# gMLP of one decoder layer: four value tiles and four u tiles computed as two Strassen units, and the value norm applied in the copy of the turned values

## The chip, the cores and the metric

The kernel runs on one core of one Trainium2 chip. A run's time is the device time of one execution in microseconds (us). The kernel before took 1926.22 us, the median of three runs (1925.88 to 1927.91). Its profile shows one execution of 1926.16 us, whose recorded span is 1924.4 us; the other 1.76 us lie around the span.

Five engines work side by side, each with its own list of instructions in a fixed order: TensorE (PE, with its weight loads PEld), VectorE (DVE), ScalarE (ACT), GpSimd (POOL) and SyncE (SP), which issues the DMAs. An instruction starts when the engine is free and the semaphores that it waits for have come.

## What is computed

Two layers over 544 tokens (512 of a prompt, 32 of eight samples) with a model width of 1024. The change lies in the token mixer of layer 0, a chunked gMLP:

```python
def rmsnorm(x, g):
    y = x * lax.rsqrt(jnp.mean(x * x, axis=-1, keepdims=True) + EPS)
    return y * g

def gmlp_mix(xn, w_in, v_norm, w_s, b_s, w_out):
    u, v = jnp.split(xn @ w_in, 2, axis=-1)
    v = rmsnorm(v, v_norm)
    ...
    ws = w_s[:, :c, :c] * mask[None]
    s = jnp.einsum('gts,bnsgd->bntgd', ws, vg)
    s = s + b_s[:, :c].T[None, None, :, :, None]
    s = s.reshape(bsz, n_ch * c, D_GMLP)[:, :L]
    return (u * s) @ w_out, v
```

`xn` is the normed residual stream, `w_in` is 1024 x 2048 (u in the first half, v in the second), chunks have 128 tokens, and the 8 groups have 128 channels each. The v rows of the samples are an output of their own (`gv`).

## The kernel before

**Layout.** Activations stand channel-major: 8 chunks of 128 channels on the partitions, 544 tokens along the row. A float32 operand is split into a high and a low part (fp32r), and a product is three matmuls: high by high (L286), high by low (L290), low by high (L292). A matmul has 128 input channels, 128 output channels and one of two interleaved halves of 272 tokens. An output chunk (`tile_mm`) is so 8 x 3 x 2 = 48 matmuls.

**Weights.** SP loads 512 KB blocks. `_split` makes the high part with an ACT cast (L242) and the low part with a DVE subtraction (L243), each 128 x 1024. How far ahead of its use a block is split, summed and loaded is `self.ahead`. The FFN stages already use Strassen's scheme: `seven` names seven pieces of a block of 2 x 2 weights, four of which are sums (L227 on DVE), `forms` makes seven forms of the activations, and `ffn_steps` multiplies each piece by its form in a step of 24 matmuls. Seven steps (168 matmuls) give what four output chunks give in 192. The results are put together from three accumulators, A (steps 1, 6, 7, 4), B (step 2) and C (steps 5, 3): after steps 1, 5 and 6 ACT copies the accumulator as it stands (L548), and DVE adds these copies to the accumulators of steps 2, 7 and 3; after step 4 ACT copies A out. A step that goes on in an accumulator waits until the copy of the step before has been read from it.

**gMLP.** `gmlp` (L605 on) runs v chunks 0 to 7, then u chunks 0 to 7, as plain tiles. The norm of x is applied behind the products: `rstd` adds up the squares over the channels with matmuls against ones (L408), takes the reciprocal root on ACT (L386) and refines it on DVE (L389 to L393); every v and u tile is multiplied by it when it leaves the accumulator (L646, L658). Each v tile is squared on ACT and added to `sq` on POOL (L369, L371). After u tile 0, `rv = self.rstd(sq)` gives the value norm, by which DVE multiplies every v tile (L661). `v_turn` turns a v tile with five transposes on PE (L667, L668) and ACT copies the turned tile out of PSUM (L670, L671); it also scales the 32 sample tokens by the gain and writes them by a DMA per tile (L663, L664). `spatial` is the product with the masked token weights (L678, L681), the gain and bias (L689, L692), the product with u (L696) and a split for the output product. Turns and spatial products stand between u tiles 1 to 7; the eight output tiles follow (L716). POOL masks the token weights at the start of the stage (L632, L634).

**Order.** The order on each engine is fixed when the program is built, from the order of the code and the priorities of its scheduler. PSUM has three buffers `ps` (two banks each) and two `pb`; a tile waits for the reader of the tile that had its buffer.

Of the kernel before, what the change touches and what calls it, by code (L numbers as in the profile page):

```python
# [25 lines left out]
AF = mybir.ActivationFunctionType  # L26
# [28 lines left out]

SEVEN = "1562734"
# [81 lines left out]
class Builder:  # L138
# [79 lines left out]
    def _sum(self):  # L218
        p = self.pieces[self.p_sum]
        self.p_sum += 1  # L220
        if p["sum"] is None:
            return
        a, op, b = p["sum"]
        get = lambda x: self._raw(x, 1024) if isinstance(x[1], int) else self.sums[x]
        a, b = get(a), get(b)
        t = self.flat(1024)
        self.nc.vector.tensor_tensor(t, a, b, ALU.add if op == "+" else ALU.subtract)  # L227
        self.sums[p["key"]] = t
# [109 lines left out]
    def prep(self, h, gcol, pair=None, cols=slice(0, T)):  # L338

        pair = self.big(F32R) if pair is None else pair  # L340
        g = self.gain(gcol)
        self.nc.scalar.activation(pair[:, 0, cols], h[:, cols], AF.Copy, scale=g)  # L342
        self.nc.vector.scalar_tensor_tensor(  # L343
            pair[:, 1, cols], h[:, cols], g, pair[:, 0, cols].bitcast(F32), ALU.mult, ALU.subtract)
        return pair

# [272 lines left out]
    def gmlp(self, h, box, on_chunk):  # L619
# [16 lines left out]
        rstd, sq, v = None, self.st(), []  # L636
        for c in range(NC_):
# [7 lines left out]
            def take(p=p, vc=vt[:, c % 2, :]):  # L645
                nc.vector.tensor_tensor(halves(vc), whole(p), halves(rstd), ALU.mult)  # L646
# [12 lines left out]

        def v_turn(c):  # L660
            nc.vector.tensor_tensor(v[c], v[c], rv, ALU.mult)  # L661
            vs = self.sm(NS)
            nc.vector.tensor_scalar(vs, v[c][:, SEQ:], self.gain(G_GV + c), None, ALU.mult)  # L663
            self.late = nc.sync.dma_start(out=self.o["gv"][c], in_=vs)  # L664
# [5 lines left out]
            nc.scalar.copy(vt[:, 0, :SEQ], t[:, 0, :])  # L670
            nc.scalar.copy(vt[:NS, 1, :P], t[:NS, 1, :P])  # L671
            vts[c] = (vt[:, 0, :], vt[:, 1, :])

# [27 lines left out]
        u_tile(0)  # L701
        rv = self.rstd(sq)
        u_tile(1)
        u_tile(2)
        assert self.chain is None
        v_turn(0)
        v_turn(1)
        for c, spatials, turns in ((3, (0,), (2, 3)), (4, (1,), (4,)), (5, (2, 3), (5,)), (6, (4, 5), (6, 7)),
                                   (7, (6, 7), ())):
# [3 lines left out]
            spatial(*spatials)  # L713
# [660 lines left out]
    def build(self):  # L1374
# [14 lines left out]
        plain([i["win"][NC_ + c] for c in range(NC_)] + [i["win"][c] for c in range(NC_)])  # L1389
# [101 lines left out]

def _constants():
# [30 lines left out]
def _arrays(x_prompt, x_sample, p_prompt, p_sample, cache_k, cache_v, cache_logf, page_table, ffn1_norm, ffn1_w1,  # L1523
# [27 lines left out]
    a["wf"] = w_kvf[:, 2 * D + head[:NS]].reshape(NC_, P, NS).transpose(1, 0, 2).reshape(P, NC_ * NS)  # L1551
    a["wq"], a["wo"] = _stationary(att_w_q[0]), _stationary(att_w_o[0])
# [46 lines left out]
```

## Time and profile before

| | before |
|---|---|
| median of three runs | 1926.22 us |
| profiled execution | 1926.16 us |
| its span | 1924.4 us |
| PE busy | 1903.1 us (99%), 16508 matmuls |
| DVE busy | 1457.2 us (76%) |
| ACT busy | 949.1 us (49%) |
| POOL busy | 142.2 us (7%) |
| v tile 0 starts on PE | 353.1 us |
| first output tile of gMLP starts on PE | 458.4 us |

The gMLP stage from v tile 0 to the first output tile takes 105 us of the span. A row of the timeline has the start, the duration, the engine, the line and the operation, then the output and inputs by their names and shapes, the number of instructions put together (x2), and in brackets the idle time ahead of it and what ended it. Recorded matmuls overlap in the pipe, so what counts on PE is the distance between starts.

### The profile page before, as it was taken

To read this page: it belongs to the slowest core of one execution; us is meant where nothing else is said; L and a number is where in the kernel's file an instruction comes from. 1 tells how busy PE (TensorE), PEld (TensorE's weight loads), DVE (VectorE), ACT (ScalarE), POOL (GpSimd) and SP (SyncE) were. 2 spreads that over 40 slices of the span, in tenths; PEclk is the share of its full clock that TensorE was granted. 3 is DMA by queue.
4 is the path that set the end of the run, shared out by engine and by line. 5 is a ranking of instruction groups with operands and counts; after the bars stand their busy time and mean duration, and the time that the engine had idled before them with its cause. 6 is when DMAs were issued, how large, how long until landed. Compare 5 with 4: busy or idle time off the path is not lost.

```text
span 1924.4 us, 39011 instructions
## 1 busy us (share of the span) xinstructions
PE 1903.1 (99%) x16508; PEld 1869.2 (97%) x16508; DVE 1457.2 (76%) x1801; ACT 949.1 (49%) x1398; POOL 142.2 (7%) x190
## 2 busy tenths in 40 slices
PE   9999999999999999999999999999999999999999
PEld 8999999999999999999999999999977899999999
DVE  7987877556788887767578887876476888878774
ACT  7544434424554544454466444444374754444461
POOL 0000000400100000023000000002131300000020
PEclk9999999999999999999999999999999999999999
DMA  5323235203223233431484232324769332332431
GB/s 197 92 98 125 88 115 165 90 26 110 89 88 116 94 113 121 130 112 50 150 304 148 97 129 71 128 96 128 227 212 333 101 109 86 107 113 86 143 106 47
DMA packets 98048, 237.62 MB, mean 123 GB/s; under 512 B 12130, under 2 KB 29826, under 8 KB 97874
## 3 DMA queue, kind: packets, MB, share of 16 engines
q1 hardware_dynamic: 97730, 235.09, 36.9%
q8 instruction: 130, 2.13, 0.5%
q14 instruction: 44, 0.36, 0.1%
q10 hardware_dynamic: 144, 0.04, 0.0%
HBM read 218.65 MB, written 16.44 MB: 122 GB/s over the span
## 4 chain that ended last, share of the span: by engine, by line
PE 89%; DVE 6%; ACT 3%; issue 1%; DMA 1%; POOL 0%; SPq 0%; ACTq 0%; DVEq 0%; POOLq 0%
PE ps L540 31%; PE ps L286 15%; PE ps L292 15%; PE ps L290 15%; PE pb L540 5%; DVE big L243 1%; ACT big L242 1%; DVE big L227 1%; PE ps L893 1%; PE ps L894 1%; PE ps L895 1%; DMA big<-in_w13p 1%; DVE big L331 0%; DVE big L498 0%; PE ps L1289 0%
## 5 line engine op out<-in xcount | busy, mean ns | idle before, releaser
L540 PE MATMUL ps<-big,big 128*128 128x272 f32 x5616 | 668.7, 279 | 4.0 <-ACT tmp L548 2.6
L540 PEld LDWEIGHTS ps<-big,big 128*128 128x128 f32 x5616 | 658.5, 189 | 5.0 <-ACT tmp L548 3.2
L243 DVE TENSOR_TENSOR big<-big,big 128x1024 fp32r<-128x1024 f32 (+2 forms) x507 | 582.3, 1152 | 87.1 <-ACT big L242 86.4
L242 ACT CAST big<-big 128x1024 fp32r<-128x1024 f32 (+2 forms) x507 | 482.5, 972 | 326.1 <-DVE big L227 253.2
L286 PE MATMUL ps<-big,big 128*128 128x272 f32 x2668 | 530.3, 280 | 3.6 <-ACT big L242 2.3
L292 PE MATMUL ps<-big,big 128*128 128x272 f32 x2668 | 527.6, 279 | 1.4 <-DVE big L243 1.3
L290 PE MATMUL ps<-big,big 128*128 128x272 f32 x2668 | 527.5, 279 | 0.5 <-DVE big L343 0.5
L286 PEld LDWEIGHTS ps<-big,big 128*128 128x128 f32 x2668 | 407.3, 189 | 8.2 <-ACT big L242 5.2
L292 PEld LDWEIGHTS ps<-big,big 128*128 128x128 f32 x2668 | 406.8, 189 | 2.8 <-DVE big L243 2.4
L290 PEld LDWEIGHTS ps<-big,big 128*128 128x128 f32 x2668 | 406.8, 189 | 0.9 <-DVE big L343 0.9
L371 POOL TENSOR_TENSOR st<-st,tmp 128x544 f32<-128x544 f32 (+1 forms) x63 | 87.6, 1391 | 1485.0 <-ACT tmp L369 1484.8
L227 DVE TENSOR_TENSOR big<-big,big 128x1024 f32<-128x1024 f32 x156 | 190.1, 1218 | 0.0
L579 DVE SCALAR_TENSOR_TENSOR big<-ps,big 128x544 f32<-128x544 f32 x128 | 92.4, 722 | 104.1 <-PE ps L292 103.2
L548 ACT COPY tmp<-ps 128x544 f32<-128x544 f32 x117 | 71.5, 611 | 111.3 <-PE ps L540 111.2
L498 DVE TENSOR_TENSOR big<-big,st 128x1088 f32<-128x1088 f32 x88 | 113.2, 1288 | 3.4 <-ACT big L562 2.0
L540 PE MATMUL pb<-big,big 128*128 128x272 f32 x936 | 114.8, 279 | 0.0
L540 PEld LDWEIGHTS pb<-big,big 128*128 128x128 f32 x936 | 111.3, 189 | 0.0
L501 ACT ACTIVATE big<-big 128x544 f32<-128x544 f32 x88 | 57.8, 659 | 87.7 <-DVE big L498 87.6
L342 ACT ACTIVATE big<-big,gains 128x544 fp32r<-128x544 f32 (+1 forms) x80 | 55.5, 702 | 90.0 <-DVE big L579 55.1
L331 DVE TENSOR_TENSOR big<-big,big 128x544 fp32r<-128x544 f32 (+1 forms) x112 | 79.3, 714 | 22.8 <-ACT big L330 22.6
L343 DVE SCALAR_TENSOR_TENSOR big<-big,gains,big 128x544 fp32r<-128x544 f32 (+1 forms) x80 | 64.7, 816 | 23.6 <-ACT big L342 23.4
L330 ACT CAST big<-big 128x544 fp32r<-128x544 f32 (+1 forms) x112 | 71.2, 644 | 12.0 <-DVE big L504 7.4
(218 smaller groups left out, 1385.8 us busy)
## 6 DMA issues: line engine op xcount, KB each, us to landing
big<-in_w SPq DMA_DIRECT2D x156, 512.0 KB
big<-in_w2b SPq DMA_DIRECT2D x96, 384.0 KB
big<-in_w13p SPq DMA_DIRECT2D x16, 512.0 KB
big<-in_w2a SPq DMA_DIRECT2D x16, 512.0 KB
big<-in_win SPq DMA_DIRECT2D x16, 512.0 KB
big<-in_wg SPq DMA_DIRECT2D x16, 512.0 KB
big<-in_ck SPq DMA_DIRECT2D x16, 512.0 KB
big<-in_cv SPq DMA_DIRECT2D x16, 512.0 KB
```

The source lines that it names most:

```text
L227: self.nc.vector.tensor_tensor(t, a, b, ALU.add if op == "+" else ALU.subtract)
L242: self.nc.scalar.copy(hi[:, c], src[:, c])
L243: self.nc.vector.tensor_tensor(lo[:, c], src[:, c], hi[:, c].bitcast(F32), ALU.subtract)
L286: i = nc.tensor.matmul(o, wh, xh[:, b], start=s, stop=False)
L290: nc.tensor.matmul(o, wh, xl[:, b], start=False, stop=False)
L292: nc.tensor.matmul(o, wl, xh[:, b], start=False, stop=e)
L331: self.nc.vector.tensor_tensor(pair[:, 1, cols], src, pair[:, 0, cols].bitcast(F32), ALU.subtract)
L371: nc.gpsimd.tensor_tensor(acc[:, cols], acc[:, cols], sq, ALU.add)
L498: tt(g, g, rstd.unsqueeze(1).broadcast_to([P, 2, T]), ALU.mult)
L540: nc.tensor.matmul(turns(dst[w]), a[:, c], woven(b), start=k in "152" and kp == 0 and n == 0, stop=kp == NKP - 1 and n == 2, skip_group_ch ...
L548: nc.scalar.copy(t["r" + k], t["C" if k == "5" else "A"])
L579: nc.vector.scalar_tensor_tensor(halves(h[c]), whole(out), 0.5, halves(h[c]), ALU.mult, ALU.add)
```

## The change

The gMLP of layer 0 gets seven forms of x for each pair of chunks (`forms`, made between v tiles 0 to 3), and its v chunks 4 to 7 and u chunks 0 to 3 become two Strassen units over them (`strassen`; weights `win7`, stacked on the host from the same `w_in`). The steps of the v unit follow v tile 3 in the order "1265734". Those of the u unit come as "126", then the statistics of the value norm, "5", "7", the new `columns`, "3", turn 0, "4", turn 1. The norm of x is multiplied in by one 128 x 1088 product for each pair of chunks (`scaled`). The value norm is no longer multiplied into the v tiles by DVE: `columns` turns `rv` into a column for each block of 128 tokens (five transposes and two small copies), and ACT applies it as a scale in the copies of the turned values, now four of 128 x 128 and one of 32 x 128 for each tile. The sample rows of v are collected in `own` and leave by one DMA.

```diff
+STEPS = "1265734"
...
-    def seven(self, aps):
+    def seven(self, aps, order=(0, 2, 3, 1)):
         r = len(self.aps)
-        self.aps.extend(aps[k] for k in (0, 2, 3, 1))
-        a11, a21, a22, a12 = ((r + k, 0) for k in range(4))
+        self.aps.extend(aps[k] for k in order)
+        a11, a12, a21, a22 = ((r + order.index(k), 0) for k in range(4))
...
+        self._form(p)
+    def _form(self, p):
+        if p["key"] in self.sums:
+            return
         a, op, b = p["sum"]
-        get = lambda x: self._raw(x, 1024) if isinstance(x[1], int) else self.sums[x]
+        def get(x):
+            if isinstance(x[1], int):
+                return self._raw(x, 1024)
+            if x not in self.sums:
+                self._form(next(y for y in self.pieces[self.p_sum:] if y["key"] == x))
+            return self.sums[x]
...
+    def strassen(self, xf, done):
+        nc, tt, t = self.nc, self.nc.vector.tensor_tensor, {}
+        u4 = lambda t: t.rearrange("p w (b a) -> p w a b", a=2)
+        h4 = lambda t: t.rearrange("p w (a b) -> p w a b", a=2)
+        def last(a):
+            done(a, t["g"][a])
+        def step(k):
+            hi, lo = self.unit()
+            self.advance()
+            if k == "1":
+                t["g"] = self.big(), self.big()
+            if k == "2":
+                t["B"] = [self.pb()[:, :HT] for _ in range(2)]
+            elif k in "15":
+                t["A" if k == "1" else "C"] = self.ps()[:, :, :HT]
+            out = t["A" if k in "1674" else "C" if k in "53" else "B"]
+            for kp in range(NKP):
+                xh, xl = xf[kp][k]
+                for n, (a, b) in enumerate(((hi, xh), (hi, xl), (lo, xh))):
+                    for w in range(2):
+                        c = slice(512 * w + P * kp, 512 * w + P * kp + P)
+                        nc.tensor.matmul(turns(out[w] if k == "2" else out[:, w]), a[:, c], woven(b),
+                                         start=k in "152" and kp == 0 and n == 0, stop=kp == NKP - 1 and n == 2,
+                                         skip_group_check=True)
+            if k in "156":
+                t["r" + k] = self.tmp().rearrange("p (w b) -> p w b", w=2)
+                nc.scalar.copy(t["r" + k], out)
+            elif k == "2":
+                for w in range(2):
+                    tt(halves(t["g"][0][:, w, :HT]), unwoven(out[w]), unwoven(t["r1"][:, w]), ALU.add)
+            elif k == "7":
+                tt(h4(t["g"][1][:, :, HT:]), u4(out), u4(t["r5"]), ALU.add)
+            elif k == "3":
+                tt(h4(t["g"][0][:, :, HT:]), u4(out), u4(t["r6"]), ALU.add)
+                last(0)
+            else:
+                nc.scalar.copy(h4(t["g"][1][:, :, :HT]), u4(out))
+                last(1)
+        return step
...
-        rstd, sq, v = None, self.st(), []
-        for c in range(NC_):
+        rstd, sq, v, xf = None, self.st(), {}, []
+        def square(c):
+            self.ssq(sq, v[c], first=c == 0)
+        for c in range(NC_ // 2):
             if rstd is None:
                 p, rstd = self.tile_rstd(xs, box["acc"])
             else:
             if c % 2 == 0:
                 vt = self.big()
-            def take(p=p, vc=vt[:, c % 2, :]):
+            def take(p=p, c=c, vc=vt[:, c % 2, :]):
                 nc.vector.tensor_tensor(halves(vc), whole(p), halves(rstd), ALU.mult)
-                self.ssq(sq, vc, first=not v)
-                v.append(vc)
+                v[c] = vc
+                square(c)
             self.evac(take)
+            xf.append(self.forms(h, G_MIX, c, xs))
+            if c == 1:
+                self.ahead = (2, 3, 6)
+        def scaled(g):
+            nc.vector.tensor_tensor(g, g, rstd.unsqueeze(1).broadcast_to([P, 2, T]), ALU.mult)
+        def v_done(a, g):
+            scaled(g)
+            for w in range(2):
+                v[NC_ // 2 + 2 * w + a] = g[:, w]
+                square(NC_ // 2 + 2 * w + a)
+        step = self.strassen(xf, v_done)
+        for k in STEPS:
+            step(k)
         m, us = [None] * NC_, {}
         vts = {}
             us[c] = us["t"][:, c % 2, :]
             nc.vector.tensor_tensor(halves(us[c]), whole(p), halves(rstd), ALU.mult)
+        own = self.tmp()
         def v_turn(c):
-            nc.vector.tensor_tensor(v[c], v[c], rv, ALU.mult)
-            vs = self.sm(NS)
-            nc.vector.tensor_scalar(vs, v[c][:, SEQ:], self.gain(G_GV + c), None, ALU.mult)
-            self.late = nc.sync.dma_start(out=self.o["gv"][c], in_=vs)
+            nc.vector.scalar_tensor_tensor(own[:, c * NS:c * NS + NS], v[c][:, SEQ:], self.gain(G_GV + c), rv[:, SEQ:],
+                                           ALU.mult, ALU.mult)
             t = self.ps()
             for j in range(4):
                 nc.tensor.transpose(t[:, 0, j * P:(j + 1) * P], v[c][:, j * P:(j + 1) * P], self.ident)
             nc.tensor.transpose(t[:NS, 1, :P], v[c][:, SEQ:], self.ident)
             vt = self.big()
-            nc.scalar.copy(vt[:, 0, :SEQ], t[:, 0, :])
-            nc.scalar.copy(vt[:NS, 1, :P], t[:NS, 1, :P])
+            for j in range(4):
+                w = slice(j * P, j * P + P)
+                nc.scalar.activation(vt[:, 0, w], t[:, 0, w], AF.Copy, scale=rc[:, j:j + 1])
+            nc.scalar.activation(vt[:NS, 1, :P], t[:NS, 1, :P], AF.Copy, scale=rc[:NS, 4:5])
             vts[c] = (vt[:, 0, :], vt[:, 1, :])
+        def columns():
+            t, rc = self.ps(), self.sm(8)
+            for j in range(4):
+                nc.tensor.transpose(t[:, 0, j * P:(j + 1) * P], rv[:, j * P:(j + 1) * P], self.ident)
+            nc.tensor.transpose(t[:NS, 1, :P], rv[:, SEQ:], self.ident)
+            nc.scalar.copy(rc[:, :4], t[:, 0, 0:512:P])
+            nc.scalar.copy(rc[:NS, 4:5], t[:NS, 1, 0:1])
+            return rc
         def spatial(*cs):
             ps = {c: self.ps() for c in cs}
...
-        u_tile(0)
+        def u_done(a, g):
+            scaled(g)
+            for w in range(2):
+                us[2 * w + a] = g[:, w]
+        step = self.strassen(xf, u_done)
+        for k in "126":
+            step(k)
         rv = self.rstd(sq)
-        u_tile(1)
-        u_tile(2)
+        step("5")
+        step("7")
         assert self.chain is None
+        rc = columns()
+        step("3")
         v_turn(0)
+        step("4")
+        self.ahead = (2, 2, 4)
         v_turn(1)
-        for c, spatials, turns in ((3, (0,), (2, 3)), (4, (1,), (4,)), (5, (2, 3), (5,)), (6, (4, 5), (6, 7)),
-                                   (7, (6, 7), ())):
+        for c, turns, groups in ((4, (2, 3), ((0,),)), (5, (4, 5), ((1,), (2,))), (6, (6, 7), ((3,), (4,))),
+                                 (7, (), ((5,), (6,), (7,)))):
             u_tile(c)
             for k in turns:
                 v_turn(k)
-            spatial(*spatials)
+                if k == NC_ - 1:
+                    self.late = nc.sync.dma_start(out=self.o["gv"].rearrange("c p t -> p c t"),
+                                                  in_=own[:, :NC_ * NS].rearrange("p (c t) -> p c t", t=NS))
+            for cs in groups:
+                spatial(*cs)
...
-        plain([i["win"][NC_ + c] for c in range(NC_)] + [i["win"][c] for c in range(NC_)])
+        plain(i["win"][NC_ + c] for c in range(NC_ // 2))
+        for n in range(2):
+            d = self.seven([i["win7"][n, x] for x in range(4)], order=(0, 1, 2, 3))
+            self.pieces.extend(d[k] for k in STEPS)
+        plain(i["win"][c] for c in range(NC_ // 2, NC_))
         plain(i["wout"][c] for c in range(NC_))
         self.ffn_pieces(1)
         ple_units(0)
```

Names in the orders below: `st` are per-token sums and norms, `big` tiles of values and split weights, `ps` and `pb` PSUM buffers, `tmp` small tiles; the number behind a name is the buffer's, so that a producer and its reader can be matched.

**PE, between u unit step 6 and step 3.** Before, the sums of the value norm stand inside u tile 1:

```order
L290 MATMUL ps596_4851<-big497_3981,big577_4711 128x272
L408 MATMUL pb589_4831<-tmp587_4827,onesr_110 128x272
L408 MATMUL pb590_4832<-tmp587_4827,onesr_110 128x272
L290 MATMUL ps596_4851<-big497_3981,big577_4711 128x272
L292 MATMUL ps596_4851<-big497_3981,big578_4712 128x272 x2
L286 MATMUL ps596_4851<-big499_3999,big577_4711 128x272 x2
L408 MATMUL pb589_4831<-tmp588_4828,onesr_110 128x272
L408 MATMUL pb590_4832<-tmp588_4828,onesr_110 128x272
L290 MATMUL ps596_4851<-big499_3999,big577_4711 128x272 x2
L292 MATMUL ps596_4851<-big499_3999,big578_4712 128x272 x2
```

Of the change, the last rows of step 6 and the first of step 7, both in accumulator A (ps622):

```order
L383 MATMUL ps622_4842<-big569_4507,big618_4836 128x272 x4
L383 MATMUL ps622_4842<-big569_4507,big619_4837 128x272 x2
L383 MATMUL ps622_4842<-big581_4584,big618_4836 128x272 x4
L383 MATMUL ps622_4842<-big581_4584,big619_4837 128x272 x2
L383 MATMUL ps622_4842<-big548_4355,big630_4905 128x272 x4
L383 MATMUL ps622_4842<-big548_4355,big631_4906 128x272 x2
```

And the last rows of step 7 with the sums between them, then the first of step 3 in accumulator C (ps644):

```order
L383 MATMUL ps622_4842<-big580_4583,big630_4905 128x272 x4
L463 MATMUL pb637_4943<-tmp635_4939,onesr_110 128x272
L463 MATMUL pb638_4944<-tmp635_4939,onesr_110 128x272
L383 MATMUL ps622_4842<-big580_4583,big631_4906 128x272 x2
L463 MATMUL pb637_4943<-tmp636_4940,onesr_110 128x272
L463 MATMUL pb638_4944<-tmp636_4940,onesr_110 128x272
L383 MATMUL ps644_4963<-big499_3999,big641_4953 128x272 x4
L383 MATMUL ps644_4963<-big499_3999,big642_4954 128x272 x2
```

The sums of the value norm (L408, now L463) have moved from the third to sixth matmul pair of a tile to the last rows ahead of step 3; step 7 stands directly behind step 6 on ps622.

**ACT, around the same place.** Before, the copies of the turned tiles follow the reciprocal roots (L386):

```order
L369 ACTIVATE tmp581_4767<-big575_4706 128x544
L403 CAST tmp587_4827<-st537_4287 128x544
L242 CAST big593_4841<-big579_4715 128x1024
L242 CAST big597_4901<-big584_4774 128x1024
L386 ACTIVATE st591_4837<-pb589_4831,eps_78 128x272
L386 ACTIVATE st591_4837<-pb590_4832,eps_78 128x272
L670 COPY big604_4968<-ps603_4962 128x512
L671 COPY big604_4968<-ps603_4962 32x128
L670 COPY big607_4981<-ps606_4975 128x512
L671 COPY big607_4981<-ps606_4975 32x128
```

Of the change (L388 copies an accumulator after a step, L441 is the reciprocal root, L756 and L757 the columns, L747 a scaled copy of turn 0):

```order
L254 CAST big630_4905<-big626_4873 128x1024
L254 CAST big641_4953<-big632_4909 128x1024
L388 COPY tmp634_4937<-ps622_4842 128x544
L458 CAST tmp635_4939<-st536_4285 128x544
L254 CAST big646_4990<-big606_4732 128x1024
L441 ACTIVATE st639_4949<-pb637_4943,eps_78 128x272
L441 ACTIVATE st639_4949<-pb638_4944,eps_78 128x272
L388 COPY tmp645_4988<-ps644_4963 128x544
L254 CAST big651_5030<-big627_4875 128x1024
L756 COPY sm650_5022<-ps649_5021 128x4
L757 COPY sm650_5022<-ps649_5021 32x1
L747 ACTIVATE big655_5069<-ps654_5063,sm650_5022 128x128 x4
```

The copy of step 6 (tmp634) stands behind the casts of the pieces for steps 7 and 3, and the copy of step 5 (tmp645) behind the two reciprocal roots.

**DVE, from the eviction of v tile 3 on.** Before:

```order
L646 TENSOR_TENSOR big564_4587<-ps569_4598,st543_4341 128x544
L646 TENSOR_TENSOR big575_4706<-ps574_4657,st543_4341 128x544
L243 TENSOR_TENSOR big578_4712<-big568_4596,big577_4711 128x1024
L243 TENSOR_TENSOR big583_4771<-big573_4655,big582_4770 128x1024
L646 TENSOR_TENSOR big575_4706<-ps580_4717,st543_4341 128x544
L404 TENSOR_TENSOR tmp588_4828<-st537_4287,tmp587_4827 128x544
```

Of the change (L705 is the eviction of v tile 3, L239 the sums for the pieces, L411 to L343 a form of x, L255 the low parts for steps 6 and 5):

```order
L705 TENSOR_TENSOR big563_4496<-ps575_4525,st542_4339 128x544
L239 TENSOR_TENSOR big573_4521<-big561_4445,big572_4519 128x1024
L239 TENSOR_TENSOR big574_4523<-big573_4521,big516_4147 128x1024
L411 TENSOR_TENSOR tmp578_4581<-big577_4578 128x544
L413 TENSOR_TENSOR tmp579_4582<-big577_4578,tmp578_4581 128x272
L414 TENSOR_TENSOR tmp579_4582<-big577_4578,tmp579_4582 128x272
L343 TENSOR_TENSOR big580_4583<-tmp578_4581,big580_4583 128x544
L343 TENSOR_TENSOR big581_4584<-tmp579_4582,big581_4584 128x544
L255 TENSOR_TENSOR big583_4593<-big574_4523,big582_4592 128x1024
L255 TENSOR_TENSOR big589_4626<-big573_4521,big588_4625 128x1024
L239 TENSOR_TENSOR big590_4629<-big516_4147,big561_4445 128x1024
```

Where two tiles' evictions had one subtraction of a weight block each between them, two sums, a form with its two splits and two low parts now follow the eviction of v tile 3.

More of the change, by code (lines that the diff above doesn't have):

```diff
@@ L1489, in _blocks, with _pairs @@
     return w.reshape(k // 256, 2, P, m // 256, 2, P).transpose(3, 4, 1, 2, 0, 5).reshape(m // 256, 4, P, k // 256, P)
+def _pairs(w):
+    h = w.shape[1] // 2
+    return np.stack([_blocks(w[:, :h]), _blocks(w[:, h:])], 3).reshape(4, P, 1024)
 def _constants():
@@ L1551, in _arrays @@
     a["wf"] = w_kvf[:, 2 * D + head[:NS]].reshape(NC_, P, NS).transpose(1, 0, 2).reshape(P, NC_ * NS)
+    a["win7"] = np.stack([_pairs(gmlp_w_in[0][:, c:c + D // 2]) for c in (D + D // 2, 0)])
     a["wq"], a["wo"] = _stationary(att_w_q[0]), _stationary(att_w_o[0])
```

## The prediction

> **What bounds the kernel now.** I read the shares and the chain on the page first, then the windows of the gMLP stage and of a stretch of the FFN, and then the chain of waits in a stretch of plain tiles.
>
> ```profile
> PE 1903.1 (99%) x16508; PEld 1869.2 (97%) x16508; DVE 1457.2 (76%) x1801; ACT 949.1 (49%) x1398; POOL 142.2 (7%) x190
> ...
> PE 89%; DVE 6%; ACT 3%; issue 1%; DMA 1%; POOL 0%; SPq 0%; ACTq 0%; DVEq 0%; POOLq 0%
> ```
>
> ```profile
> 353.00:458.00 105.00, 105.00 (x896) 103.72 (x895) 58.91 (x83) 34.45 (x54) 18.64 (x24) 1.00 0.21 69
> 600.00:640.00 40.00, 40.00 (x348) 40.00 (x347) 37.25 (x42) 22.15 (x31) 0.00 (x0) 1.00 0.34 108
> ```
>
> ```profile
> 344.70 0.23 PE ps L292 x2
> 344.93 0.23 PE ps L286 x2
> ```
>
> In the stage that is changed (353 to 458 us; columns PE, PEld, DVE, ACT, POOL, granted clock, DMA share) PE never stops, while DVE is busy 58.9 of 105 us, ACT 34.5 and POOL 18.6. So every matmul less is worth its distance, 0.23 / 2 = 0.116 us, as long as the others keep up. The FFN, which already runs Strassen steps, shows 348 matmuls in 40 us, so a step's matmuls come as close as a tile's; but there DVE is at 37.25 of 40, and POOL does nothing.
>
> **What goes.** Two units of 168 matmuls stand for eight tiles of 48: 48 matmuls less, 48 x 0.116 = **-5.56 us**. `columns` adds five transposes:
>
> ```profile
> 415.20 0.60 PE L667 MATMUL ps<-consts,big 128*128 128x128 f32 x4
> 415.63 0.27 PE L668 MATMUL ps<-consts,big 128*32 128x128 f32 x1
> 415.74 0.60 PE L667 MATMUL ps<-consts,big 128*128 128x128 f32 x4
> 415.94 0.59 ACT L670 COPY big<-ps 128x512 f32<-128x512 f32 x1 [9.99 <-PE ps L668]
> 416.43 0.25 ACT L671 COPY big<-ps 32x128 f32<-32x128 f32 x1
> ```
>
> From one turn to the next on PE is 415.74 - 415.20 = 0.54 us, so +0.54, and **-5.0 us** in all if PE still never stops. Weight bytes stay the same, one DMA for `gv` in place of eight lies where the DMA share is 0.21, and the eight multiplications by the value norm leave a DVE that wasn't waited for. The rest of the prediction is what PE now waits for.
>
> **Three waits that the order makes for certain.** Step 7 goes on in the accumulator that ACT must first copy after step 6, directly behind it (the copies to tmp634 in the order). The FFN has such places:
>
> ```profile
> 1555.56 1.04 ACT L242 CAST big<-big 128x1024 fp32r<-128x1024 f32 x1 [1.92 <-DVE big L227]
> 1556.51 0.60 ACT L548 COPY tmp<-ps 128x544 f32<-128x544 f32 x1
> 1557.17 3.05 PE L540 MATMUL ps<-big,big 128*128 128x272 f32 x24 [1.30 <-ACT tmp L548]
> ...
> 60.25 0.96 PE L540 MATMUL ps<-big,big 128*128 128x272 f32 x6 [0.89 <-ACT tmp L548]
> ```
>
> 0.89 with ACT nearly free, 1.30 with a late cast ahead of the copy. The changed order puts a cast that waits for a DVE sum ahead of it: **1.2 us**.
>
> Step 3 needs the copy of step 5, which stands on ACT behind two reciprocal roots, and these wait for the sums that PE runs directly ahead of step 3:
>
> ```profile
> 404.77 0.40 PE L408 MATMUL pb<-tmp,onesr 128*128 128x272 f32 x2
> 405.09 0.86 ACT L386 ACTIVATE st<-pb,eps 128x272 f32<-128x272 f32 x2 [1.36 <-PE pb L408]
> ```
>
> PE is free again 0.23 after the sums start, the roots begin 0.32 after it and take 0.80 to the next start, the copy 0.60, the release 0.06 (1557.17 - 1556.51 - 0.60): 0.09 + 0.80 + 0.60 + 0.06 = **1.55 us**. Before, tile 1's remaining 40 matmuls covered the roots.
>
> The first u tile behind the turns needs the PSUM buffer of turn 0, the third one back. The scaled copies have no row; the nearest is an ACT scale out of PSUM of 128 x 256:
>
> ```profile
> L899 ACT ACTIVATE big<-ps,sm 128x256 f32<-128x256 f32 x4 | 1.6, 474 | 5.1 <-PE ps L895 5.1
> ```
>
> Four pieces by that are 1.6 with the tail, against 0.49 to the next start for one copy of 128 x 512; bounds for a turn are so 0.64 us (416.58, the next turn's first copy, less 415.94) and 1.6 + 0.25. I take 1.75, as 128 columns are below the row's 256. Copies begin 0.20 after a turn's last matmul is issued (415.94 - 415.63 - 0.11); PE has a pair (0.23) and turn 1 (0.54) in between: 0.20 + 1.75 - 0.77 = 1.2 at most, 0.1 at least: **1.0 us**. Later turns have a tile of 5.57 us between them, which hides them.
>
> ```profile
> 416.58 0.57 ACT L670 COPY big<-ps 128x512 f32<-128x512 f32 x1
> ```
>
> These three are 3.75 us.
>
> **The load on DVE and ACT.** The steps need more: eight sums, six more low parts, four forms with their splits. Prices from start to start:
>
> ```profile
> 404.46 2.35 DVE L243 TENSOR_TENSOR big<-big,big 128x1024 fp32r<-128x1024 f32 x2
> ...
> 485.47 0.44 DVE L358 TENSOR_TENSOR tmp<-big,tmp 128x272 f32<-128x272 f32 x1
> 485.94 0.44 DVE L359 TENSOR_TENSOR tmp<-big,tmp 128x272 f32<-128x272 f32 x1
> 486.30 0.72 DVE L331 TENSOR_TENSOR big<-tmp,big 128x544 fp32r<-128x544 f32 x1
> 486.94 0.72 DVE L716 TENSOR_TENSOR big<-ps,big 128x544 f32<-128x544 f32 x1
> ```
>
> ```profile
> L227 DVE TENSOR_TENSOR big<-big,big 128x1024 f32<-128x1024 f32 x156 | 190.1, 1218 | 0.0
> L498 DVE TENSOR_TENSOR big<-big,st 128x1088 f32<-128x1088 f32 x88 | 113.2, 1288 | 3.4 <-ACT big L562 2.0
> L330 ACT CAST big<-big 128x544 fp32r<-128x544 f32 (+1 forms) x112 | 71.2, 644 | 12.0 <-DVE big L504 7.4
> ```
>
> A sum or a low part takes 1.14 (two take 2.35, one 1.22), a 544 subtraction or eviction 0.64, a 272 one 0.47 and 0.36, a 1088 product 1.2; on ACT a big cast 0.95 (1555.56 to 1556.51), a small one 0.56.
>
> *First place, steps 6 and 5 of the v unit.* A v tile costs DVE eviction 0.64, form 0.64 + 0.47 + 0.36 + 2 x 0.64, low part 1.14: 4.53 of PE's 48 x 0.116 = 5.57. Tile 0 starts on PE at 353.1 and can't be evicted before the norm of x is there; that was at 364.2:
>
> ```profile
> 353.11 0.40 PE L286 MATMUL ps<-big,big 128*128 128x272 f32 x2
> ...
> 364.20 1.42 DVE L646 TENSOR_TENSOR big<-ps,st 128x544 f32<-128x544 f32 x2
> ```
>
> Now a form stands ahead of it, 366.2 at best. To v tile 3's eviction DVE has three evictions, two forms, two low parts: 9.7, and some 1.3 of waits for ACT's casts: 377.2, against the tile's end on PE at 353.1 + 4 x 5.57 + 0.46 for sums = 375.9. Then eviction, two sums, the form's first subtraction (3.56 in all), and on ACT a small cast, step 1's copy, another small cast and the cast for step 6 (0.56 + 0.53 + 0.56 + 1.04 = 2.7): 383.5. PE is through steps 1 and 2 at 375.9 + 5.57 = 381.4 and waits 2.2 with the releases, and 0.5 more after four matmuls for the cast for step 5: **2.7 us**.
>
> *Second place, the low part for step 5 of the u unit.* From step 6 above PE has 172 matmuls to it, 20.4 us with the 0.5. DVE has nine low parts and four sums (13 x 1.14), four evictions (2.0) and two products (2.4): 19.2, with some 1.5 of waits 20.7: **0.5 us**.
>
> So without anything else PE waits 3.75 + 2.7 + 0.5 = 6.95 us, and -5.0 + 6.95 = **+1.95**.
>
> **What POOL takes from DVE.** The rows of the adds of squares (L371) speak against these prices:
>
> ```profile
> 356.35 1.59 DVE L243 TENSOR_TENSOR big<-big,big 128x1024 fp32r<-128x1024 f32 x1 [0.71 <-ACT big L242]
> ...
> 358.91 3.83 POOL L632 TENSOR_TENSOR big<-big,tmp 128x128 f32<-128x128 f32 x8
> ...
> 371.10 1.22 DVE L243 TENSOR_TENSOR big<-big,big 128x1024 fp32r<-128x1024 f32 x1
> 372.07 1.44 POOL L371 TENSOR_TENSOR st<-st,tmp 128x544 f32<-128x544 f32 x1 [4.12 <-ACT tmp L369]
> 372.90 1.70 DVE L243 TENSOR_TENSOR big<-big,big 128x1024 fp32r<-128x1024 f32 x1 [0.59 <-ACT big L242]
> 377.63 1.35 POOL L371 TENSOR_TENSOR st<-st,tmp 128x544 f32<-128x544 f32 x1 [4.12 <-ACT tmp L369]
> ...
> 482.52 0.79 DVE L343 SCALAR_TENSOR_TENSOR big<-big,gains,big 128x544 fp32r<-128x544 f32 x1 [0.82 <-ACT big L342]
> ...
> 488.77 1.86 POOL L371 TENSOR_TENSOR st<-st,tmp 128x544 f32<-128x544 f32 x1 [3.92 <-ACT tmp L369]
> 489.34 1.87 DVE L343 SCALAR_TENSOR_TENSOR big<-big,gains,big 128x544 fp32r<-128x544 f32 x1
> ```
>
> An add takes 1.35 alone. A DVE instruction with two SBUF operands that starts during it is longer by about what the add has left: 1.70 for 1.22, and 1.87 for 0.79 where DVE is dense. Before, DVE had idle time around the adds; now seven stand among dense work of this kind, each at 1.1 (the dense row) to 1.35. [...]
>
> In the v tiles this takes the 1.0 us of slack (4.53 + 1.1 = 5.6 against 5.57): the masks (3.83 us of POOL over the first form and low part, of which one instruction shows 1.59 for 1.22; I take 1.1) and two adds (2.2) push v tile 3's eviction from 377.2 to 380.5, step 2, due at 375.9 + 2.8 = 378.7, after four matmuls (0.5) waits for the low part that ends as that eviction begins, 1.3 to 1.4 late, and v tile 3's own add falls on the sums, 1.1 more: step 6 starts at 388.1, 5.3 behind PE's 382.8; with the 0.5, the first place is 1.4 + 5.3 + 0.5 = 7.2. In the second, three adds of 1.23 lie ahead of the low part: 20.7 + 3.7 = 24.4 to 24.8 against 20.4: 4.2. The fourth makes step 7 wait 2.4 in place of 1.2. Sum: 7.2 + 4.2 + 2.4 + 1.55 + 1.0 = 16.35, so -5.0 + 16.35 = **+11.35**.
>
> Between +1.95 and +11.35 I go by nine tenths of the way, since the dense row shows the hold nearly whole and one sparse row (0.48) less: **+10.4 us**. The profiled execution of 1926.16 is 0.06 from the median, so 1926.2 + 10.4 = **1936.6 us**.
>
> **Rivals.** *DVE keeps up* (not slower). If adds slip into DVE's waits for casts, none of the 9.4 us between the two sums arises: 1926.2 + 1.95 = 1928.2, no change. For it: in 377.63 an add met no DVE instruction at all. Against it: the v tiles leave DVE 1.0 us per tile, less than an add. It decides from where PE's waits stay below 5.0 + 3.85 = 8.9 us, 0.2% being 3.85 us, about what a measurement of this kernel can tell from no change.
>
> *Only the certain waits, or less* (faster). With no lateness 1926.2 - 5.0 + 3.75 = 1925.0; to be faster by over 0.2% PE may wait 1.15 us in all, less than the wait at step 3 alone. With none it is 1921.2. I see nothing for it but an error in how I read the order.
>
> [...]
>
> *The change doesn't save what it says:* the count of the orders, 48 matmuls less, and the FFN's 348 in 40 us leave no room for that.
>
> **Chances.** The holds count, 1931 to 1939: 0.62, with its own range. The clock as well, up to 1941: 0.08. DVE keeps up or half so, 1922.4 to 1930: 0.22. Faster: 0.08. Slower is 0.62 + 0.08 = 0.70. The range runs from 1926 (the bounds of the turn's copies and of step 7 below 1928.2 included) to 1941.
>
> **What would show it.** Right: PE's waits of 4 us or more ahead of step 6 of the first unit and in step 5 of the second, with DVE low parts or sums of 1.7 to 2.5 us beside POOL adds; 1.5 us ahead of step 3, led by the roots; 1 us ahead of u tile 4; 48 matmuls less. Wrong: the same DVE instructions at 1.2 beside adds, or the adds starting late in DVE's gaps; then the time is near 1928. [...]

## The result and the profile after

The changed kernel took 1938.05 us (median of six runs, 1937.72 to 1939.71) against 1926.66 us for the kernel before in the same comparison: a ratio of 1.006, with a 95% interval of 1.0048 to 1.0072. It is 11.4 us slower; 10.4 was forecast. The profiled execution took 1937.72 us, its span 1935.7 (1924.4 before).

The page of the changed kernel, shares and chain:

```profile
PE 1904.7 (98%) x16465; PEld 1869.0 (97%) x16465; DVE 1488.3 (77%) x1831; ACT 974.6 (50%) x1454; POOL 148.0 (8%) x190
...
PE 71%; DVE 5%; ACT 2%; issue 1%; DMA 1%; POOL 0%; ACTq 0%; DVEq 0%; SPq 0%; POOLq 0%
```

PE has 43 matmuls fewer and yet 1.6 us more busy time (in part slower matmuls, below), and its share of the chain fell from 89% to 71%. What PE waits for in the stage, in the timeline with the idle time in brackets:

```profile
379.88 2.58 PE L383 MATMUL pb<-big,big 128*128 128x272 f32 x20 [0.53 <-DVE big L255]
387.25 19.18 PE L383 MATMUL ps<-big,big 128*128 128x272 f32 x144 [4.79 <-ACT big L254]
412.19 7.03 PE L383 MATMUL ps<-big,big 128*128 128x272 f32 x44 [2.52 <-DVE big L255]
419.93 2.81 PE L383 MATMUL ps<-big,big 128*128 128x272 f32 x22 [0.70 <-ACT tmp L388]
424.78 5.48 PE L383 MATMUL ps<-big,big 128*128 128x272 f32 x45 [1.34 <-ACT tmp L388]
```

Before, the stage had no such row. They are steps 2 and 6 of the v unit and steps 5, 7 and 3 of the u unit; a sixth, 0.73, is u tile 4. The time in brackets starts at the recorded end of the last matmul, 0.28 us after its start, and the next could have started after 0.116: each wait costs PE 0.16 more than its bracket.

DVE and POOL of the changed kernel in this stretch:

```profile
380.37 3.51 DVE L239 TENSOR_TENSOR big<-big,big 128x1024 f32<-128x1024 f32 x2
...
387.23 2.36 DVE L255 TENSOR_TENSOR big<-big,big 128x1024 fp32r<-128x1024 f32 x2 [0.22 <-ACT big L254]
...
381.29 1.50 POOL L426 TENSOR_TENSOR st<-st,tmp 128x544 f32<-128x544 f32 x1 [4.65 <-ACT tmp L424]
406.07 9.56 POOL L426 TENSOR_TENSOR st<-st,tmp 128x544 f32<-128x544 f32 x4 [23.27 <-ACT tmp L424]
...
407.49 4.65 DVE L255 TENSOR_TENSOR big<-big,big 128x1024 fp32r<-128x1024 f32 x2
412.06 2.35 DVE L239 TENSOR_TENSOR big<-big,big 128x1024 f32<-128x1024 f32 x1
```

The two sums behind v tile 3 take 3.51 us, where two low parts of the same shape take 2.36 at 387.23; the pair of low parts for u steps 6 and 5, whose end u step 5 waits for, takes 4.65, and the sum behind it 2.35 in place of 1.22. Beside each lies an add of POOL's: four of them, 1.35 alone, take 9.56 us in this stretch.

Windows of half a microsecond around the first two long waits (columns as before: PE, PEld, DVE, ACT, POOL, granted clock, DMA share):

```profile
384.50:385.00 0.50, 0.00 (x0) 0.00 (x0) 0.40 (x2) 0.45 (x1) 0.00 (x0) 0.99 0.00 0
385.00:385.50 0.50, 0.00 (x0) 0.00 (x0) 0.47 (x3) 0.50 (x2) 0.00 (x0) 0.50 0.00 0
391.50:392.00 0.50, 0.50 (x5) 0.50 (x4) 0.11 (x1) 0.36 (x1) 0.00 (x0) 0.69 1.01 410
412.00:412.50 0.50, 0.31 (x1) 0.31 (x2) 0.50 (x2) 0.00 (x0) 0.50 (x1) 0.79 0.00 0
415.50:416.00 0.50, 0.50 (x5) 0.50 (x5) 0.47 (x1) 0.00 (x0) 0.12 (x1) 0.79 0.06 25
```

The granted clock falls to 0.50 at 385.0 and is back at 391.8 (0.69 is 0.62 of the window at half); it falls again at 412.3 until 415.7. So the clock came in as well, to which the chances gave 0.08. In these stretches 172 matmuls from 387.25 took 2.3 us more than 172 x 0.116, and 44 from 412.19 took 1.8 more.

### The profile page after: what moved, and what is told of

It is laid out like the page before. It is cut to its first block, busy times and chain, and to the rows that moved or that the text cites. A ratio compares the mean times of both kernels' runs of the same rounds, so it can differ in the third digit from the quotient of the medians.

```text
span 1935.7 us, 38989 instructions
## 1 busy us (share of the span) xinstructions
PE 1904.7 (98%) x16465; PEld 1869.0 (97%) x16465; DVE 1488.3 (77%) x1831; ACT 974.6 (50%) x1454; POOL 148.0 (8%) x190
## 4 chain that ended last, share of the span: by engine, by line
PE 71%; DVE 5%; ACT 2%; issue 1%; DMA 1%; POOL 0%; ACTq 0%; DVEq 0%; SPq 0%; POOLq 0%
PE ps L595 24%; PE ps L298 12%; PE ps L304 12%; PE ps L302 12%; PE pb L595 4%; DVE big L255 2%; PE ps L383 1%; PE ps L994 1%; PE ps L995 1%; PE ps L996 1%; DVE big L239 1%; ACT big L254 1%; PE ps L1390 0%; PE ps L764 0%; DMA big<-in_cv 0%
## 5 line engine op out<-in xcount | busy, mean ns | idle before, releaser
L595 PE MATMUL ps<-big,big 128*128 128x272 f32 x5616 | 668.7, 279 | 4.0 <-ACT tmp L603 2.6
L595 PEld LDWEIGHTS ps<-big,big 128*128 128x128 f32 x5616 | 658.5, 189 | 5.0 <-ACT tmp L603 3.2
L255 DVE TENSOR_TENSOR big<-big,big 128x1024 fp32r<-128x1024 f32 (+2 forms) x513 | 590.3, 1154 | 93.2 <-ACT big L254 92.3
L254 ACT CAST big<-big 128x1024 fp32r<-128x1024 f32 (+2 forms) x513 | 488.6, 973 | 336.5 <-DVE big L239 261.8
L298 PE MATMUL ps<-big,big 128*128 128x272 f32 x2540 | 504.8, 280 | 4.0 <-ACT big L254 1.4
L304 PE MATMUL ps<-big,big 128*128 128x272 f32 x2540 | 502.2, 279 | 1.1 <-DVE big L255 1.1
L302 PE MATMUL ps<-big,big 128*128 128x272 f32 x2540 | 501.4, 279 | 0.3 <-DVE big L355 0.3
L298 PEld LDWEIGHTS ps<-big,big 128*128 128x128 f32 x2540 | 387.8, 189 | 8.9 <-ACT big L254 4.6
L304 PEld LDWEIGHTS ps<-big,big 128*128 128x128 f32 x2540 | 387.1, 189 | 2.4 <-DVE big L255 1.9
L302 PEld LDWEIGHTS ps<-big,big 128*128 128x128 f32 x2540 | 387.1, 189 | 0.5 <-DVE big L355 0.5
L426 POOL TENSOR_TENSOR st<-st,tmp 128x544 f32<-128x544 f32 (+1 forms) x63 | 91.7, 1455 | 1492.0 <-ACT tmp L424 1491.5
L239 DVE TENSOR_TENSOR big<-big,big 128x1024 f32<-128x1024 f32 x164 | 202.0, 1232 | 0.0
L343 DVE TENSOR_TENSOR big<-big,big 128x544 fp32r<-128x544 f32 (+1 forms) x112 | 79.3, 714 | 22.8 <-ACT big L342 22.6
L355 DVE SCALAR_TENSOR_TENSOR big<-big,gains,big 128x544 fp32r<-128x544 f32 (+1 forms) x80 | 64.5, 817 | 23.3 <-ACT big L354 23.3
```

What stands on the lines that cost most here:

```text
L254: self.nc.scalar.copy(hi[:, c], src[:, c])
L255: self.nc.vector.tensor_tensor(lo[:, c], src[:, c], hi[:, c].bitcast(F32), ALU.subtract)
L298: i = nc.tensor.matmul(o, wh, xh[:, b], start=s, stop=False)
L302: nc.tensor.matmul(o, wh, xl[:, b], start=False, stop=False)
L304: nc.tensor.matmul(o, wl, xh[:, b], start=False, stop=e)
L343: self.nc.vector.tensor_tensor(pair[:, 1, cols], src, pair[:, 0, cols].bitcast(F32), ALU.subtract)
```

## The experiments

Theory A: POOL's adds hold DVE, DVE is late with sums and low parts, and PE waits for it. Theory B: DVE and ACT have too much to do even without the adds. C and D are about the clock: by C a slow clock costs its whole time, by D a slow PE only waits less at the next place.

**e1: the adds left out; e2: the adds on DVE.** In `ssq`, for the v tiles alone:

```diff
-            nc.gpsimd.tensor_tensor(acc[:, cols], acc[:, cols], sq, ALU.add)
+            if add != "none":
+                (nc.vector if add == "dve" else nc.gpsimd).tensor_tensor(acc[:, cols], acc[:, cols], sq, ALU.add)
```

> Leaves out POOL's seven adds of the squares of v tiles 1 to 7 (the value norm is made from tile 0 alone); ACT's squares stay. Theory A (POOL's adds hold DVE, and DVE's lateness is what PE waits for): in the changed kernel's trace the adds lengthen DVE instructions by 1.0 to 1.2 us each, two ahead of v tile 3's eviction, one on the sums, three ahead of the low part for u step 5. Without them the wait ahead of step 6 falls from 4.8 to 1.6 us, that in u step 5 from 2.5 to about 1, the clock stays at 1.00 (it lost 3.8 us in two stretches); together 6 to 8.5 us less: 1929.5 to 1932. Theory B (the added sums, forms and low parts alone are too much for DVE and ACT, the adds fit into gaps): within 1.5 us of the change, 1936.5 to 1938.5.

> The same seven adds made by DVE in place of POOL, nothing left out. An add of 544 costs DVE 0.64 us, less than the 1.0 to 1.2 us that a POOL add holds it. Theory A: DVE gains 3 us up to u step 5, the waits shrink by as much and part of the slow clock's 3.8 us goes: 1932 to 1935.5. Theory B: DVE has 7 x 0.64 = 4.5 us more to do and the waits grow: 1940 to 1943.

e1 took 1931.08 us (before: 1926.67 in this comparison; ratio 1.0023, 1.0013 to 1.0032), 7.0 less than the change and inside Theory A's range. Its sums behind v tile 3, in the timeline:

```profile
378.28 2.47 DVE L239 TENSOR_TENSOR big<-big,big 128x1024 f32<-128x1024 f32 x2
```

2.47 for 3.51. The wait ahead of step 6 fell to 2.86, not to 1.6, and the clock still fell there, to 0.50 for 3.4 us. e2 took 1930.56 (1.002, 1.001 to 1.0029), 7.5 less, although DVE does the seven adds itself: more than the 2.5 to 6 expected. Its waits:

```profile
PE ps L383 <- ACT big L254: 3.8, 1, 3.8
PE ps L383 <- ACT tmp L388: 1.3, 1, 1.3
PE pb L383 <- DVE big L255: 0.5, 1, 0.5
```

Those of u steps 5 and 7 and of u tile 4 are gone altogether. Theory B falls: seven adds of 0.64 us on DVE cost less than what they cost DVE from POOL, about 1.1 each by the rows above.

But e2's edit also changed the order that the program was built with. Of the change:

```profile
422.81 0.40 PE L383 MATMUL ps<-big,big 128*128 128x272 f32 x2
431.22 0.48 PE L383 MATMUL ps<-big,big 128*128 128x272 f32 x2
432.98 0.50 PE L298 MATMUL ps<-big,big 128*128 128x272 f32 x2 [0.73 <-ACT big L748]
```

Of e2:

```profile
414.54 2.48 PE L383 MATMUL ps<-big,big 128*128 128x272 f32 x20
425.82 0.48 PE L298 MATMUL ps<-big,big 128*128 128x272 f32 x2
```

Between the two pairs of the norm's sums lie two matmuls in the change and 20 in e2; the last two matmuls of step 4 stand between turns 0 and 1 in the change and ahead of the columns in e2, and u tile 4 starts there without a wait. On ACT the copy of step 6 stands behind two late casts in the change (at 414.45 and 417.98) and behind one in e2 (410.38). So of e2's gain the waits of u step 7 and u tile 4, 1.8 us together (the table below), may be the order's. e1 has the change's order on DVE and ACT, keeps both waits (0.89 and 0.73) and is still 7.0 faster: it is the clean test of the adds.

**e3: another order in the u unit.**

```diff
-        for k in "126":
+        for k in "1562":
             step(k)
         rv = self.rstd(sq)
-        step("5")
         step("7")
         assert self.chain is None
-        rc = columns()
         step("3")
+        rc = columns()
...
-            self.pieces.extend(d[k] for k in STEPS)
+            self.pieces.extend(d[k] for k in (STEPS, SEVEN)[n])
```

> The u unit in the FFN's order of pieces (1562734), the statistics of the value norm behind step 2 and the columns behind step 3; all else as in the change. If the waits ahead of u steps 7 and 3 (0.7 and 1.3 us) come from the order on ACT (copies behind late casts and behind the reciprocal roots), both go: 2 us less, 1936. If DVE's lateness sets when the u unit ends, the wait appears in another step and the time stays at 1938.

1937.02 us (1.0051, 1.0034 to 1.0068), between the two: 1.0 less. Its waits:

```profile
PE ps L383 <- ACT big L254: 4.8, 1, 4.8
PE pb L383 <- DVE big L255: 4.3, 2, 3.8
PE ps L754 <- ACT big L398: 0.9, 1, 0.9
PE ps L383 <- ACT tmp L388: 0.2, 1, 0.2
```

The waits of steps 7 and 3 went as expected, but u step 2 now waits 3.8 for a low part: what the order saves, DVE's lateness mostly takes back.

**e4: work for PE where it stood idle.** Ahead of step 6 of the v unit:

```diff
-            elif k in "15":
+            elif k in "15" and not (k == "5" and "C" in t):
...
+            t["w" + k] = hi
+            if k == "6" and fill:
+                t["C"] = self.ps()[:, :, :HT]
+                for n in range(fill):
+                    nc.tensor.matmul(turns(t["C"][:, n % 2]), t["w2"][:, :P], woven(xf[0]["2"][0]), start=True, stop=True)
```

> 36 matmuls of nothing (4.2 us of PE, results thrown away) right ahead of step 6 of the v unit, where PE waits for 4.8 us. Theory C (the granted clock fell to 0.50 because PE stood idle there, and the lost 2.2 us count in full): the clock reads 1.00 behind step 6 and the time is 2.2 us lower, 1935.9. Theory D (DVE's lateness is the bound up to u step 5; a PE at half clock only waits less there): the clock reads 1.00, but the wait in u step 5 grows by about 2 us, and the time stays within 0.7 us of 1938.

1937.79 us (1.0057, 1.004 to 1.0074), against 1938.05. PE's waits in the profiled execution:

```profile
387.23 0.73 PE L388 MATMUL ps<-big,big 128*128 128x272 f32 x4 [0.62 <-ACT big L254]
...
410.54 5.36 PE L388 MATMUL ps<-big,big 128*128 128x272 f32 x44 [2.52 <-DVE big L255]
417.93 2.82 PE L388 MATMUL ps<-big,big 128*128 128x272 f32 x22 [2.03 <-ACT tmp L393]
```

Step 6 begins at 387.23, as in the change (387.25), and the clock reads 1.00 there and, in this execution, in u step 5 too. That step resumes 1.65 us earlier than in the change (410.54 for 412.19): from step 6 to there DVE stands idle for 1.6 us, behind casts, in place of 3.2; the wait there is the same, 2.52, and step 7 waits 2.03 in place of 0.70. So in this execution the full clock was worth about 2 us of the 4.1 that the slow stretches took, and the rest came back as waiting. It took 1936.43; the other three, with a mean clock of 0.998 to 0.999, took 1937.33 to 1938.38. By the median Theory D is nearer, by this trace the truth lies between C and D; four runs that scatter over 2 us don't settle the share.

**e5, e11: a plain u tile ahead of the v unit, with the adds on DVE (e5) and on POOL (e11).** The turns and spatial products then lie around u tiles 5 to 7; the pieces in `build` follow.

```diff
+        u_tile(NC_ // 2)
         step = self.strassen(xf, v_done)
...
-        for c, turns, groups in ((4, (2, 3), ((0,),)), (5, (4, 5), ((1,), (2,))), (6, (6, 7), ((3,), (4,))),
-                                 (7, (), ((5,), (6,), (7,)))):
+        for c, turns, groups in ((5, (2, 3), ((0,),)), (6, (4, 5), ((1,), (2,))),
+                                 (7, (6, 7), ((3,), (4,), (5,), (6,), (7,)))):
```

> Adds on DVE as in e2, and u tile 4 as a plain tile between v tile 3 and the v unit (turns 2 to 7 and the spatial products then lie around u tiles 5 to 7). Theory A (PE waits because DVE is late for the first unit's sums and low parts): the tile gives PE 5.57 us of work there and DVE only 1.8, so the waits ahead of steps 2 and 6 of the v unit (0.5 and 3.8 in e2) and the slow clock behind them (2.2) go, 5 to 6.5 us less than e2: 1924 to 1926, up to 1 more if the turns then lack cover. Rival (DVE and ACT have too much over the whole stage): the waits only move behind, 1929 to 1931.

> The change with u tile 4 ahead of the v unit, POOL's adds as in the change. Theory A (both the adds' holds and the lack of cover make DVE late, and PE's waits are their difference): the cover takes 3.7 us off the first unit's 5.3 and with it the slow clock there, but DVE stays 3 us later than in e5: 1928 to 1931. If the cover alone is enough, as e5: 1925 to 1926.

e5 took 1925.26 us against 1926.44 (0.9996, 0.9986 to 1.0006), no difference from before and 5.3 less than e2, as Theory A had it. e11 took 1934.07 (1.0038, 1.0024 to 1.0051): 8.8 more than e5, and more than the 3 to 6 expected. The edit is the engine of seven adds, but in the u unit e11 has the change's order and e5 that of e2. In the two traces PE's waits in the stage differ by 6.5 us (from start to start), of which u step 7 and u tile 4 are 3.1 and may be the order's; where the rest of the 8.8 lies these traces don't show. Low parts for u steps 6 and 5 in e11, with POOL's four adds, and in e5:

```profile
408.02 9.56 POOL L426 TENSOR_TENSOR st<-st,tmp 128x544 f32<-128x544 f32 x4 [23.88 <-ACT tmp L424]
...
409.49 4.59 DVE L255 TENSOR_TENSOR big<-big,big 128x1024 fp32r<-128x1024 f32 x2
```

```profile
406.32 0.71 DVE L427 TENSOR_TENSOR st<-st,tmp 128x544 f32<-128x544 f32 x1
406.96 1.22 DVE L255 TENSOR_TENSOR big<-big,big 128x1024 fp32r<-128x1024 f32 x1
408.10 0.71 DVE L427 TENSOR_TENSOR st<-st,tmp 128x544 f32<-128x544 f32 x1
408.73 1.22 DVE L255 TENSOR_TENSOR big<-big,big 128x1024 fp32r<-128x1024 f32 x1
```

In e11 the cover took most of the wait ahead of step 6 of the first unit (0.89 is left; ahead of and in step 2 it has 0.95 and 0.53), but the four adds of the v unit fall on the low parts for the u unit all the same, 2.52 in step 5 and 2.04 in step 7: the u tile ahead doesn't reach there.

**e12: the adds on DVE in the kernel before.**

> The kernel before with the seven adds of the v tiles' squares on DVE in place of POOL, as in e2. If the adds' engine matters only where DVE's work is what PE waits for (Theory A), it changes nothing here, where PE never waits: within 1 us of before. If DVE adds are worth time by themselves, as the step from e11 to e5 (8.8 us) could also be read, several us less than before.

1927.12 against 1926.36 (1.0004, 0.9995 to 1.0014): no difference that shows. The adds' engine mattered where PE waited for DVE (7.5 us from the change to e2, a part of it perhaps the order's), and not here, where it doesn't.

**e6, e9, e10: the rest of e5's waits.** e6 gives e5 the u unit's order of e3; e9 moves `rv = self.rstd(sq)` behind `step("5")`; e10 is e9 with u tiles 4 and 5 both ahead of the v unit.

> e5 with the u unit in the order 1562734, the statistics behind step 2 and the columns behind step 3. Now that DVE isn't late, the wait of step 3 for the copy behind the reciprocal roots (1.3 in e2) goes: 1 to 1.3 us less than e5, 1923 to 1925. If e5's u unit has no such wait any more, the same time as e5.

> e5 with the statistics of the value norm behind step 5 of the u unit in the code: ACT's copy of step 5 then stands ahead of the reciprocal roots, and the sums on PE between steps 7 and 3. If e5's wait of 1.3 us ahead of step 3 is the copy's place on ACT, it goes, and steps 3 and 4 (5.6 us) cover the roots for the columns: 1.3 us less than e5, about 1924, faster than before by 2 us or more. Rival (the roots are then late for the columns instead): the wait moves there, 1925 to 1926.

> As e9, with u tiles 4 and 5 both ahead of the v unit. The remaining waits of the first unit in e5 (0.3, 0.9, 0.2) go, 1.4 less; but only u tiles 6 and 7 are left around turns 2 to 7, whose scaled copies take ACT 1.8 us a turn: the last turns and spatial products are then uncovered, 1 to 4 us more. Sum 1923 to 1927, likeliest 1925.

e6 took 1928.73 (1.0012, 1.0003 to 1.0022), 3.5 more than e5, a miss. The wait of step 3 went, and a longer one came where the columns need the refined norm:

```profile
426.92 0.63 PE L756 MATMUL ps<-consts,st 128*128 128x128 f32 x4 [2.75 <-issue]
```

The step of the refinement that ends it stands on DVE behind two 1088 products (1.28 and 1.29 us). e9 took 1924.99 (0.9993, 0.9984 to 1.0002). The wait of 1.34 ahead of step 3 is gone from its trace and 0.18 at the columns is new, but its median is only 0.3 below e5's, where 1.3 was expected; the two times aren't told apart. e10 took 1924.25 against 1926.45 (0.9989, 0.998 to 0.9998): the one version that is faster than before, by 0.1%, with an interval that ends just short of 1. Its waits:

```profile
PE ps L757 <- ACT big L398: 1.1, 1, 1.1
PE ps L767 <- DVE tmp L781: 1.1, 1, 1.1
PE ps L383 <- ACT tmp L388: 0.5, 1, 0.5
```

Nothing is left ahead of the v unit, and 2.2 us have come to the columns and to the spatial products, which two u tiles no longer cover.

**e7: the value norm's part alone; e8: the u unit alone.** e7 is the kernel before with `columns`, the scaled copies and the one DMA; in e8 v tiles 0 to 7 are plain and the forms stand behind v tiles 4 to 7.

> The kernel before with the second part of the change alone: columns, the value norm as ACT's scale in the copies of the turned values, one DMA for gv; no Strassen unit. Five transposes (0.54) and the wait for a PSUM buffer at the next u tile (0.7 in the change's trace): 1.2 us more than before, 1927.9. If the four copies in place of one make each of the four later groups of turns wait as well, 3 us or more: 1929.5 and above. If the eight DVE products that go were worth time, no more than before.

> The change with the u unit alone: v tiles 0 to 7 plain, the forms behind v tiles 4 to 7, POOL's adds as they were; 24 matmuls less in place of 48: 2.8 less, 0.54 more for the columns. Theory A: the unit still has forms, sums and two adds ahead of it, the wait ahead of its step 6 is 2 to 4 us, and 2 us in steps 3 and u tile 4: 1928 to 1931. Rival (it takes two units in a row to make DVE late): only the 2 us, 1926 to 1927.

e7 took 1926.83 against 1926.44 (1.0005, 0.9995 to 1.0014), and its stage has no row of waits: by the trace the second part costs the 0.5 of its transposes. The wait of 0.7 at the next u tile, which was expected, isn't there, so four scaled copies in place of one don't make it by themselves. e8 took 1931.07 (1.0026, 1.0015 to 1.0037), 4.6 more than before with 24 matmuls fewer; the unit's step 6 waits again, and the clock falls behind it, to 0.50 for 3.4 us:

```profile
PE ps L383 <- ACT big L254: 3.9, 1, 3.9
PE ps L298 <- ACT big L746: 0.7, 1, 0.7
PE ps L383 <- ACT tmp L388: 0.4, 1, 0.4
```

It doesn't take two units: here and in the change the unit that comes first, behind four forms with their splits and with POOL's adds, finds DVE late.

## Why the prediction held, and where its sizes were off

The terms, in us of PE's time (a stretch from start to start, less 0.116 for each of its matmuls; 5.05 is 387.25 - 379.88 - 20 x 0.116):

| term | forecast | measured |
|---|---|---|
| 48 matmuls less, `columns` | -5.0 | -5.0 (count) |
| v unit, steps 2, 6 and 5 | 7.2 | 0.26 + 0.80 + 5.05 = 6.1 |
| u step 5, low part | 4.2 | 2.7 |
| u step 7, copy of step 6 | 2.4 | 0.9 |
| u step 3, copy behind the roots | 1.55 | 1.5 |
| u tile 4, buffer of turn 0 | 1.0 | 0.9 |
| slow clock | 0 | 2.3 + 1.8 = 4.1 |
| sum | +11.35, taken at 10.4 | +11.2 |

The spans differ by 11.3, so the measured terms close the account within their rounding.

*Three waits that the order makes for certain.* All three came, at the places named, with 0.9, 1.5 and 0.9 us. Nearest to certain was that of step 3, which stays at 1.34 in e1, e2, e4, e5 and e11 (0.42 in e8). Those of u step 7 and u tile 4 are gone in e2, where the scheduler made another order of the same code, and e7 has none at its u tile. Ahead of step 3 the chain is the one worked out, sums, roots, copy, matmul:

```profile
423.04 0.40 PE L463 MATMUL pb<-tmp,onesr 128*128 128x272 f32 x2
423.36 0.87 ACT L441 ACTIVATE st<-pb,eps 128x272 f32<-128x272 f32 x2 [1.99 <-PE pb L463]
424.12 0.61 ACT L388 COPY tmp<-ps 128x544 f32<-128x544 f32 x1
424.78 0.38 PE L383 MATMUL ps<-big,big 128*128 128x272 f32 x1 [1.34 <-ACT tmp L388]
```

e9 takes this wait away by putting the copy ahead of the roots on ACT, which shows that it was the order.

*What POOL takes from DVE.* The step that decided the forecast, that the adds hold DVE and PE pays for it, is shown: e1 leaves the adds out and 7.0 us go with them. e2 and the pair e5 and e11 move them to DVE, and 7.5 and 8.8 go, a part of which may be the order's. The forecast gave them 8.5, nine tenths of 9.4, with no slow clock in it; in e1 and e2 some of the gain is a slow clock that got shorter (3.4 and 6.8 us at 0.50, against 10.2 in the change). The DVE rows beside adds are longer by 1.15 (3.51 for 2.36, or 1.04 against e1's 2.47), 2.3 (4.65 for 2.36, two adds) and 1.1 (2.35 for 1.22), about 0.8 of the 1.35 for each add.

*The load without the adds* was priced at +1.95. e1, which has none, is 4.4 above before: its first unit waited 2.86 where 2.2 was worked out, and the clock, which the sum left out, fell there for 3.4 us.

*Mis-sized terms.* The three waits that hang on DVE's lateness were forecast at 13.8 together and measured at 9.7, and the slow clock, which the sum left out, at 4.1. The two belong together in part: in the change PE, at 0.50 in u step 5, came later to step 7 and waited 0.7 there; where the clock stayed at 1.00 behind u step 5, in e4 and e11, step 7 waits 2.0, near the forecast's 2.4. The rest is size: in e4, with the full clock, DVE takes 23.3 us from step 6 to the low part of u step 5 (410.54 - 387.23), where 24.4 to 24.8 were worked out. So the mechanism was right, and that the sum came so near is luck in this part: two errors nearly cancel, waits too long and a clock taken as constant. For the clock as well the chances have a time up to 1941; no run shows such a cost on top of the waits. The runs showed 4.1 us of slow clock in the change, of which about 2 counted in e4's profiled execution.

*DVE keeps up* and *only the certain waits* didn't come true for the change. e5 shows where the first would have: with a u tile ahead of the unit and the adds on DVE, PE's waits fall to 4.3, counted as in the table, and the time is that of before.

## What to carry to other kernels

Fewer matmuls paid here only where the other engines had room for what the scheme adds (48 less took 11.4 us more in the change and 2.2 less in e10): price its sums, forms and splits per tile against the matmul time of the tile, and look first at what has to be ready for the first step. A small add on POOL beside dense two-operand work on DVE cost more here than the same add on DVE itself (leaving seven out gained 7.0 us, putting them on DVE 7.5); where PE didn't wait for DVE no gain showed (e12, 1927.12 against 1926.36). An edit of one engine's work can also change the order that the program is built with, so compare the orders before a difference is put down to the edit. The slow clock behind the long waits wasn't simply added to them: of its 4.1 us in the change about half was time that PE, at full clock in e4's profiled execution, waited at later places.

## What the runs showed of the hardware

In this stage the granted clock fell to 0.50 at waits of 4.79 and 2.52 us in the change, 2.86 in e1, 3.8 in e2, 4.8 and 3.8 in e3, 2.75 in e6 and 3.9 in e8. In the change it fell 2.5 us after PE's last matmul ended (382.46 to 384.99) and 2.6 (409.67 to 412.29); in e4 and e11 waits of 2.52 left it at 1.00. In e6 it fell at 428.15, when PE had already worked again for 1.2 us after its wait of 2.75:

```profile
428.00:428.50 0.50, 0.50 (x5) 0.50 (x4) 0.24 (x2) 0.20 (x1) 0.00 (x0) 0.65 0.00 0
```

The slow stretches have two lengths: 3.4 us in the change (412.29 to 415.71), e1, e6 and e8, and 6.8 in the change (384.99 to 391.81), e2 and, twice, e3. What sets the lengths, and why the same wait of 2.52 ended both ways, no run shows.
